# Two stretches of a decoder step written out as lists of steps: from the pool mixer to the second half layer's first Strassen tile, with a third plain tile, and from attention's end to the last half layer's first one

## The chip, the cores and the metric

The kernel runs on one core of one Trainium2 chip. The metric is the device time of one execution in microseconds (us); lower is better. Three runs of the kernel before the change took 1669.02, 1671.43 and 1675.51 us; their median is 1671.43 us.

## The reference, cut to what matters

One inference step of a small decoder: 512 prompt tokens and 8 sample tokens (520 columns), width 1024, hidden width 2816, two layers. Each layer is half a SwiGLU channel mixer, a token mixer, and another half channel mixer, each behind its own root-mean-square norm:

```python
x = x + 0.5 * _swiglu(_rmsnorm(x, norm_g[l, 0]), ffn_w_gate[l, 0], ffn_w_up[l, 0], ffn_w_down[l, 0])
h = _rmsnorm(x, norm_g[l, 1])
# layer 0: out = causal means of h over windows 2, 4, 8, 16, less h, times pool_w, times pool_scale
# layer 1: out = sliding-window attention with sinks on shared keys and values, times w_o
x = x + out
x = x + 0.5 * _swiglu(_rmsnorm(x, norm_g[l, 2]), ffn_w_gate[l, 1], ffn_w_up[l, 1], ffn_w_down[l, 1])
```

So there are four "half layers" (channel mixers), numbered 0 to 3; the pool mixer stands between 0 and 1, the shared keys and values and half layer 2 follow 1, and attention stands between 2 and 3. Outputs are the final norm of x and the new caches. Everything is float32.

## The kernel before, in words

**Layout and precision.** x is kept transposed: eight tiles of 128 channels by 520 tokens. Each float32 operand of a product is split into a high part in TensorE's faster format and the rest as a low part (ScalarE copies the high part, VectorE subtracts: L192 and L193 for weights, L345 and L346, L348 and L349 for activations). Each product is then three matmuls (L519, L545): high by high, high by low, low by high. The norm's factor per token is not applied to x but to the result, as a row R that is multiplied in later, so products can begin before the norm is known.

**A half layer** (`ffn`, L672) makes 22 tiles of 128 hidden channels in three parts of 8, 8 and 6 (`PARTS`), and after each part multiplies with the down weights and adds into x (L711, L712). A hidden tile is gate times up. The first `NPL[fi]` tiles of half layer fi are plain (`plain_tile`, L577): 8 blocks of 128 channels, 3 terms, gate and up, 2 halves of the tokens, which makes 96 matmuls. The others are Strassen tiles (`strassen_tile`, L614): gate and up for both halves of the channels are taken as seven products of 12 matmuls, 84 in all. A Strassen tile needs sums of the weights (two accumulating DMAs from GpSimd's queue, L156 and L157, and two VectorE adds, L162 and L166) and sums of the activations (`sums`, L649: four t12 and four t34 tiles, each split again at L345 and L346). The activations' sums are made once per half layer, while its plain tiles are multiplied; the first Strassen tile waits for them. `NPL` is (3, 2, 2, 2).

**Weights** (`Weights`, L96) come in chunks of 1 MB through three buffers, by DMAs on SyncE's queue (L359). A chunk's buffer is free when all its items are split. `prefetch` (L233) splits five items ahead.

**Start of a half layer.** Half layers 1 and 3 start with `start_hooks` (L732): after each group of four blocks a hook is called, which in turn sums the squares over channels with matmuls against ones (`rstd_tok`, L477), takes the root on VectorE in 12 short instructions (`root`, L486), spreads it over the partitions (`rstd_all`, L500), and makes the activations' sums step by step. `copied` and `known` (L569, L571) copy a plain tile out of PSUM where R is not yet there.

**Pool mixer** (L1008 to L1102). For each of four channel groups, five token blocks are multiplied with pool_w (`zt`, 30 matmuls at L1029), scaled by the norm and split (`zt_evac`, L1033; the scale needs the root), and multiplied with band matrices that hold the means' windows (`band`, L1040, 22 matmuls and 4 short ones). The result goes into x (L1064 for samples, L1067 for the prompt), and x, scaled, is split into the next half layer's operand. The squares for the next norm come after the last group, and eight transposes (L1097) make the pool's state for the output. The sum of squares for the mixer's own norm must hold x of all eight blocks, and the last comes out of half layer 0's last down product.

**Order.** Outside of lists, the framework places instructions by its own timeline estimate, each engine in one in-order queue. Attention, the very beginning and the very end are already written as lists: a `Steps` object (L237) takes steps with an engine, a cost, a due time, what they come after, and which buffer slots they take; it plans them by those numbers, and inside `manual_schedule` the steps go out in exactly that order on TensorE, VectorE, ScalarE and GpSimd. The planner's numbers fix the order and nothing else: on the chip each queue waits for what it needs.

Of the kernel before, what the change touches and what calls it, by code (L numbers as in the profile page):

```python
# [11 lines left out]
F32 = mybir.dt.float32  # L12
# [18 lines left out]
NPL = (3, 2, 2, 2)  # L31
# [64 lines left out]
class Weights:  # L96
# [4 lines left out]
    def __init__(self, nc, rawp, splp, chunks_ahead, ahead):  # L101
        self.nc, self.rawp, self.splp = nc, rawp, splp
        self.ca, self.ahead = chunks_ahead, ahead
        self.chunks, self.items = [], []
        self.nl = self.na = self.ns = self.ng = 0
        self.late = None

# [34 lines left out]
    def sums(self, ch, again):  # L142
# [28 lines left out]
        self.last()  # L171
        self.piece(ch, s2)
        self.piece(ch, lambda raw: blk(raw, 1, 2))
        self.piece(ch, s4)
# [24 lines left out]

    def hi(self, new=None):  # L200
# [3 lines left out]
        src = it[1](self.chunks[it[0]][1])  # L204
# [14 lines left out]
        def ahead(i=self.ns):  # L219
            held = any(c < it[0] for c, _, _ in self.items[i + 1 : i + 3])  # L220
            self.load(it[0] + self.ca - held)
            self.add_up(it[0] + 1)
# [81 lines left out]
def yoco_step(ctx, tc, ins, outs):  # L304
# [148 lines left out]
    N_KV, N_FIN, N_PS = 6, 7, 8  # L453
    r_tok = cp.tile([P, 8], F32, name="r_tok")
# [217 lines left out]
    def ffn(fi, tmp, mov, hooks, tt, tags, after, before_last=None, given=None, end=None):  # L672

        j = 0
        for pi, n in enumerate(PARTS):
            last = pi == len(PARTS) - 1
            hs = Hidden(tags)
            for _ in range(n):
                if given is not None:
                    given(hs)  # L680
                    given = None
                elif j < NPL[fi]:
# [10 lines left out]
            for m0 in range(0, KT, 2):  # L693
# [13 lines left out]
                for m in (m0, m0 + 1):  # L707
# [5 lines left out]
                    if last:  # L713
                        if before_last is not None:
                            next(before_last, None)
                        after(m)

# [3 lines left out]
    def deferred(n, tmp, tag, tags, lst, w=TOK):  # L721


        def f(k):
            z = pair(tags, [P, w])
            split(tuple(a[:, :TOK] for a in z), x[k], gcol(n, k))
            lst.append(z)
            square(k, tmp, tag)
# [22 lines left out]
    with ff_pool() as tmp:  # L751
# [174 lines left out]
        def first_tile(hs):  # L926
# [8 lines left out]
            copied.append(rest)  # L935

# [22 lines left out]
        sel = cp.tile([P, 34], F32, name="sel")  # L959
        sts = cp.tile([P, KT, NS], F32, name="sts")  # L960
# [45 lines left out]
        ffn(0, tmp, mov0, first_hooks(), tt, HH, deferred(1, tmp, "g", XX, mov1, TW), pool_prep(), first_tile)  # L1006

    with tc.tile_pool(name="pm", bufs=2) as pm:  # L1008
        for k in range(KT):
            split(tuple(z[:, TOK:TW] for z in mov1[k]), sts[:, k, :])  # L1010

        tok0 = (0, 128, 256, 384, 400)
        r5 = pm.tile([P, 1], F32, name="r5", bufs=1)

        def zt(gi):

            pd = duo()
            banks = [pd[:, 0, :], pd[:, 1, :], ps()]
            wh, wl = prep["w", gi]
            views = []  # L1020
            for tau in range(5):
                o = banks[tau // 2][:, (tau % 2) * 256 : (tau % 2) * 256 + 256]
                views.append(o)
                n = 0
                for kk in range(2):
                    xh, xl = mov1[2 * gi + kk]
                    s = slice(tok0[tau], tok0[tau] + P)
                    for a, b in ((xh, wh), (xh, wl), (xl, wh)):
                        T.matmul(o, a[:, s], b[:, kk, :], start=(n == 0), stop=(n == 5))  # L1029
                        n += 1  # L1030
            return views

        def zt_evac(views):  # L1033
            zh = pm.tile([P, 5, 256], F32R, tag="zh", name="zh")
            zl = pm.tile([P, 5, 256], F32R, tag="zl", name="zl")
            for tau in range(5):
                split((zh[:, tau, :], zl[:, tau, :]), views[tau], r_tok[:, tau : tau + 1] if tau < 4 else r5)
            return zh, zl

        def band(gi, zz):  # L1040

            zh, zl = zz
            Gt, (th, tl) = prep["G", gi], (prep["T", gi][:, 0, :], prep["T", gi][:, 1, :])
            G = lambda c: Gt[:, B_G + c : B_G + c + 256]
            for mi in range(2):
                m = 2 * gi + mi
                c = slice(mi * P, (mi + 1) * P)
                pd = duo()
                po, pso = pd[:, 0, :], pd[:, 1, :]
                pl = [(0, zh, th), (0, zl, th), (0, zh, tl), (1, zh, G(0)), (1, zl, G(0))]  # L1050
                pr = [(1, zh, G(256)), (1, zl, G(256)), (2, zh, G(128)), (2, zl, G(128)), (3, zh, G(0)), (3, zl, G(0))]
                for half, lst in ((0, pl), (1, pr)):
                    for i, (tau, z, b) in enumerate(lst):
                        T.matmul(  # L1054
                            po[:, half * 256 : half * 256 + 256],
                            z[:, tau, c],
                            b,
                            start=(i == 0),
                            stop=(i == len(lst) - 1),
                        )  # L1060
                bs = Gt[:, B_S : B_S + NS]
                T.matmul(pso[:, :NS], zh[:, 4, c], bs, start=True, stop=False)
                T.matmul(pso[:, :NS], zl[:, 4, c], bs, start=False, stop=True)
                V.scalar_tensor_tensor(  # L1064
                    x[m][:, SP:], pso[:, :NS], gcol(N_PS, m), x[m][:, SP:], op0=ALU.mult, op1=ALU.add
                )
                V.scalar_tensor_tensor(  # L1067
                    x[m][:, :SP], po, gcol(N_PS, m), x[m][:, :SP], op0=ALU.mult, op1=ALU.add
                )
# [889 lines left out]
```

## Time and profile before

| | |
|---|---|
| median of 3 runs | 1671.43 us (1669.02 to 1675.51) |
| the profiled execution's own time | 1674.94 us |
| its span, first to last instruction | 1673.1 us |
| its granted TensorE clock | 0.992 of full |
| DVE, ACT and POOL busy | 1254.4, 884.6 and 175.2 us |
| HBM over the span | 111 GB/s |

In the profile PE is TensorE, PEld its weight loads, DVE VectorE, ACT ScalarE, POOL GpSimd and SP SyncE; a q behind the name is the engine's queue of waits and DMA issues. A row "engine line <- other line: 3.4, 1, 3.4" means 3.4 us of waiting in total, once, 3.4 at the longest. The table of windows gives for each stretch its length, the busy time of each engine with the number of instructions, the granted TensorE clock (PEclk), the busy share of the DMA engines and GB/s. The chain of waits lists pieces as start, length, engine, tile, line and count. "ps" is any pair of PSUM banks; "wh" and "wl" are a weight item's high and low part, "th" and "tl" those of the activations' sums.

### The profile page before, as it was taken

The page shows a single profiled execution, that of the slowest core. Times are in us where ns is not written, and L with a number is a line of the kernel's source. Part 1 is how long each engine was busy: PE and PEld are TensorE (multiplying, and loading weights), DVE is VectorE, ACT ScalarE, POOL GpSimd, SP SyncE. Part 2 cuts the span into 40 slices and gives each one's busy share as a digit, 9 for nine tenths or more (in the row PEclk, how much of TensorE's full clock was granted, in tenths as well). Part 3 has the DMA queues.
Part 4 walks back from the last instruction along what each step waited for, and adds up shares of the span by engine and source line. Part 5 has one row for each costly group of instructions (what it writes and reads, how often), then busy time and mean ns, then how long its engine had stood idle before and what let it go on. Part 6 is the DMA issues. An engine that isn't in the chain of part 4 may idle for free.

```text
span 1673.1 us, 34561 instructions
## 1 busy us (share of the span) xinstructions
PE 1647.5 (98%) x13802; PEld 1629.3 (97%) x13802; DVE 1254.4 (75%) x2400; ACT 884.6 (53%) x1763; POOL 175.2 (10%) x235
## 2 busy tenths in 40 slices
PE   9999999999899999999999999999999999999997
PEld 9999999999899999999999999999989999999997
DVE  7966866887785785878785785778987785785785
ACT  6643643656662562556562562555875663463463
POOL 1101101000101101100201110100220110110100
PEclk9999999999999999999999999999999999999999
DMA  9546846753466665633666666654142565675641
GB/s 241 133 132 135 182 132 136 175 161 97 93 162 152 139 162 145 142 108 114 154 157 156 135 154 162 139 147 113 27 102 71 112 160 143 141 171 137 141 115 52
DMA packets 318240, 227.08 MB, mean 136 GB/s; under 512 B 9568, under 2 KB 293336, under 8 KB 318038
## 3 DMA queue, kind: packets, MB, share of 16 engines
q1 hardware_dynamic: 291360, 178.50, 38.4%
q0 software_dynamic: 23392, 41.83, 15.5%
q10 hardware_dynamic: 3326, 4.53, 0.9%
q8 instruction: 108, 1.77, 0.4%
q14 instruction: 54, 0.44, 0.1%
HBM read 180.89 MB, written 5.04 MB: 111 GB/s over the span
## 4 chain that ended last, share of the span: by engine, by line
PE 93%; DVE 4%; ACT 1%; DMA 1%; issue 1%; DVEq 0%; ACTq 0%
PE ps L545 47%; PE ps L519 32%; PE pa L519 5%; PE ps L1780 2%; PE p L519 1%; PE pb L1385 1%; PE pc L1456 1%; PE ps L1029 1%; PE pc L1441 1%; DMA pr<-in_bands_dram 1%; PE ps L1054 1%; DVE wl L193 1%; PE ps L483 0%; PE t L809 0%; ACT wh L192 0%
## 5 line engine op out<-in xcount | busy, mean ns | idle before, releaser
L192 ACT ACTIVATE wh<-raw 128x512 fp32r<-128x512 f32 (+1 forms) x690 | 418.1, 622 | 511.4 <-PE ps L519 294.2
L193 DVE TENSOR_TENSOR wl<-raw,wh 128x512 fp32r<-128x512 f32 (+1 forms) x690 | 456.6, 677 | 193.1 <-ACT wh L192 189.5
L545 PE MATMUL ps<-th,wh 128*128 128x260 f32 x1264 | 358.5, 284 | 3.6 <-ACT th L345 1.7
L545 PE MATMUL ps<-tl,wh 128*128 128x260 f32 x1264 | 358.1, 284 | 0.6 <-DVE tl L346 0.6
L545 PE MATMUL ps<-th,wl 128*128 128x260 f32 x1264 | 356.4, 284 | 0.8 <-DVE wl L193 0.8
L545 PEld LDWEIGHTS ps<-th,wh 128*128 128x128 f32 x1264 | 238.9, 189 | 5.0 <-ACT th L345 2.1
L545 PEld LDWEIGHTS ps<-tl,wh 128*128 128x128 f32 x1264 | 239.3, 189 | 1.0 <-DVE tl L346 1.0
L545 PEld LDWEIGHTS ps<-th,wl 128*128 128x128 f32 x1264 | 238.4, 189 | 1.2 <-DVE wl L193 1.2
L519 PE MATMUL ps<-hh,wh 128*128 128x260 f32 x1024 | 206.6, 283 | 0.6 <-ACT vtok L1207 0.6
L519 PE MATMUL ps<-hl,wh 128*128 128x260 f32 x1024 | 207.1, 282 | 0.0
L519 PE MATMUL ps<-hh,wl 128*128 128x260 f32 x1024 | 205.1, 282 | 0.0
L545 PE MATMUL ps<-xh,wh 128*128 128x260 f32 x708 | 199.1, 284 | 2.0 <-ACT wh L192 1.5
L545 PE MATMUL ps<-xl,wh 128*128 128x260 f32 x708 | 198.7, 283 | 0.0
L157 POOL DMA_DIRECT2D raw<-raw x79 | 68.4, 866 | 1241.7 <-DVE wl L193 566.5
L545 PE MATMUL ps<-xh,wl 128*128 128x260 f32 x708 | 195.3, 283 | 1.4 <-DVE wl L193 1.4
L519 PEld LDWEIGHTS ps<-hl,wh 128*128 128x128 f32 x1024 | 158.4, 188 | 0.0
L519 PEld LDWEIGHTS ps<-hh,wh 128*128 128x128 f32 x1024 | 157.0, 188 | 1.0 <-ACT vtok L1207 0.9
L519 PEld LDWEIGHTS ps<-hh,wl 128*128 128x128 f32 x1024 | 157.4, 188 | 0.0
L545 PEld LDWEIGHTS ps<-xh,wh 128*128 128x128 f32 x708 | 133.7, 189 | 2.7 <-ACT wh L192 1.9
L711 DVE TENSOR_TENSOR u<-ps,R 128x520 f32<-128x520 f32 x88 | 61.3, 697 | 97.1 <-PE ps L519 97.1
L545 PEld LDWEIGHTS ps<-xl,wh 128*128 128x128 f32 x708 | 133.8, 189 | 0.0
L545 PEld LDWEIGHTS ps<-xh,wl 128*128 128x128 f32 x708 | 131.8, 189 | 1.8 <-DVE wl L193 1.8
(299 smaller groups left out, 3247.1 us busy)
## 6 DMA issues: line engine op xcount, KB each, us to landing
raw<-in_ffn_w_gate_dram SPq DMA_DIRECT2D x87, 512.0 KB
raw<-in_ffn_w_up_dram SPq DMA_DIRECT2D x87, 512.0 KB
raw<-in_ffn_w_down_dram SPq DMA_DIRECT2D x32, 1024.0 KB
S<-in_ffn_w_up_dram SPq DMA_DIRECT2D x79, 256.0 KB
raw<-raw POOLq DMA_DIRECT2D x79, 256.0 KB, 3.3
S<-raw POOLq DMA_DIRECT2D x79, 256.0 KB, 4.6
raw<-in_ffn_w_down_dram SPq DMA_DIRECT2D x16, 768.0 KB
raw<-in_w_q_dram SPq DMA_DIRECT2D x8, 512.0 KB
```

Of the source, the lines that this page charges most:

```text
L157: G.dma_start(blk(raw, 2, 1), blk(raw, 1, 1), accum_op=ALU.add)
L192: nc.scalar.activation(dh, src, AF.Copy)
L193: nc.vector.tensor_tensor(dl, src, dh.bitcast(F32), op=ALU.subtract)
L519: T.matmul(banks[:, hf, :H], a[:, kk, :], hcols(b, hf), start=(first and i == 0), stop=(last and i == 2),)
L545: T.matmul(bank[:, :H], a[:, kk, :], b, start=(not more and kk == 0 and i == 0), stop=(kk == 3 and i == 2), skip_group_check=more,)
L711: V.tensor_tensor(halves(u), banks[m][:, :, :H], halves(R), op=ALU.mult)
L1029: T.matmul(o, a[:, s], b[:, kk, :], start=(n == 0), stop=(n == 5))
L1054: T.matmul(po[:, half * 256 : half * 256 + 256], z[:, tau, c], b, start=(i == 0), stop=(i == len(lst) - 1),)
L1385: T.matmul(o, q_[rows_, qc], k_[rows_, kc_], start=(i == 0), stop=(i == 2))
L1441: T.transpose(pt[:, o : o + P], vals["sm", t, h, bi][:, e, kt * P : (kt + 1) * P], ident)
L1456: T.matmul(po[rows_, bi * P : (bi + 1) * P], vtok[:, max(b - 1, 0) + kt, v0 : v0 + 64], vals["pp", t, h, bi][:, kt * 256 + e * P : kt * 25 ...
L1780: T.matmul(bank, a[:, k % 3, :], b[:, c0:c1], start=(k == 0 and i == 0), stop=(k == 5 and i == 2))
```

## The change

It does six things.

1. `NPL` becomes (3, 3, 2, 2): half layer 1 has a third plain tile in place of its first Strassen tile.
2. Half layer 0 stops two output blocks early (`stop=6`); those two (m = 6 and 7) become the first steps of a new list. `pool_prep` is advanced twice after m = 4 and m = 5, so that its eight steps still fit.
3. The list holds the two output blocks, the whole pool mixer, the norm and sums for half layer 1, its three plain tiles and the first six of seven products of its first Strassen tile. In it, the mixer's sum of squares takes x of block 7 straight from its square (ten sum matmuls in place of five); the four z groups are multiplied with their order and PSUM places fixed; the band product of a block is one run of 520 columns with one addition into x; the first plain tile alternates gate and up for each channel block k, as soon as that block's operand is split.
4. `begin` (shared by both lists) takes the root with one GpSimd instruction (`pow`) in place of the 12 on VectorE, and writes the activations' sums as single steps. `weight_steps` writes the weight items as steps: the accumulating DMAs (`wa`) come behind the norm's root on GpSimd's queue, and the two VectorE adds become steps of their own (`look`).
5. The last half layer starts with a second list: a Silu call that brings in the activation table first, then `begin` with two plain tiles and six products.
6. The DMAs that copy state and caches in DRAM and load the sinks (one of 448 KB, two of 1016 KB, 17 small ones, on SyncE's queue) are issued before the first list in place of after the pool mixer.

The diff's core:

```diff
-NPL = (3, 2, 2, 2)
+NPL = (3, 3, 2, 2)
...
+            done = 0
+            if given is not None:
+                done = given(hs)
+                given = None
+                j += done
+            for _ in range(n - done):
+                if j < NPL[fi]:
...
-            for m0 in range(0, KT, 2):
+            for m0 in range(0, stop if last else KT, 2):
...
                             next(before_last, None)
+                            if stop < KT and m >= stop - 2:
+                                next(before_last, None)
...
+    def weight_steps(st, first, have, count, due, gate=(), width=lambda i: 4):
...
+            add(f"wa{c}", "POOL", 2.2, due(heads[c][0]) - 4.0, lambda c=c: W.add_up(c), after=after + list(gate))
...
+            if first + i in W.made:
+                add(f"ws{i}", "DVE", 0.14 * n + 0.13, due(i) - 0.2, lambda i=i: W.look(first + i), after=after)
+                after = after + [f"ws{i}"]
+            add(f"wh{i}", "ACT", 0.13 * n + 0.13, due(i) - 0.1, lambda i=i: w_hi(i), after=after, takes=takes)
+            add(f"wl{i}", "DVE", 0.14 * n + 0.13, due(i), lambda i=i: w_lo(i), after=[f"wh{i}"] + ([f"wl{i - 1}"] if i else []))
...
+    def begin(st, fi, n, mov, tmp, tt, first, off, base, need, ready, summed, hidden_list, root_):
...
+        def n_root():
+            nc.gpsimd.tensor_tensor(r_tok[:, :5], vals["v"], minus_half, op=ALU.pow)
...
+        for p in range(npl):
+            order = [(k, o) for k in range(KT) for o in range(2)]
+            if p:
+                order = [(k, o) for k0 in (0, 4) for o in range(2) for k in range(k0, k0 + 4)]
...
+        ups, los = [f"L{k}1" for k in range(4)], [f"L{k}0" for k in range(4)]
+        extra = {0: [f"p{npl - 1}.71"], 1: los + ["s0"], 2: ["cs0", "s1"], 3: ["s2"], 4: ["cs1", "s3"], 5: ["cs2", "s4"] + ups}
...
-        ffn(0, tmp, mov0, first_hooks(), tt, HH, deferred(1, tmp, "g", XX, mov1, TW), pool_prep(), first_tile)
+        hs0 = ffn(0, tmp, mov0, first_hooks(), tt, HH, deferred(1, tmp, "g", XX, mov1, TW), pool_prep(), first_tile, stop=6)
...
+        st = Steps(dict(d=4, w=6, sb=4, sa=2, g=2, t=2, sq=2))
...
+        add("x5", "DVE", 3.0, -100.0)
+        add("y5", "ACT", 2.5, -100.0)
...
+                T.matmul(o, acc[:, lo : lo + P], ones[:, 0:1], start=True, stop=False)
+                T.matmul(o, vals["q", 1, 7][:, lo : lo + P], ones[:, 0:1], start=False, stop=True)
...
+        add("ns", "PE", 1.25, 10.5, norm_sums, after=["q7", "a6"], takes=("d",), reads=[("sq", "q7")])
+        add("nm", "DVE", 0.17, 11.0, norm_mean, after=["ns"], reads=[("d", "ns")])
+        add("nr", "POOL", 1.4, 11.0, norm_root, after=["nm"])
...
-        ffn(1, tmp, mov2, start_hooks(tmp, 2, tt, 2), tt, HH, deferred(N_KV, tmp, "g", XX, movk))
+        ffn(1, tmp, mov2, [], tt, HH, deferred(N_KV, tmp, "g", XX, movk), given=mixed)
...
-        ffn(3, tmp, mov6, start_hooks(tmp, 5, tt, 1), tt, HH, None, end=last_part)
+            st.add("tab", "ACT", 1.4, -50.0, table)
...
+        ffn(3, tmp, mov6, [], tt, HH, None, given=first_part, end=last_part)
```

In the lists, x5 and y5 stand for what VectorE and ScalarE still have queued when the first list begins. PSUM is four pairs of banks (d=4). `s0` to `s5` are the Strassen products: s1 waits for the low parts of all four t12 (L00 to L30), s5 for those of all four t34.

More of the change, by code (lines that the diff above doesn't have):

```diff
@@ L727, in f @@
             lst.append(z)
+            if w > TOK:
+                split(tuple(a[:, TOK:] for a in z), sts[:, k, :])
             square(k, tmp, tag)
@@ L935, in first_tile @@
             copied.append(rest)
+            return 1
         def first_hooks():
@@ new lines, in yoco_step, with mixed @@
+        add("ht", "PE", 0.95, 30.0, h_turn, after=[f"hx{k}" for k in range(KT)], takes=("d",))
+        for a in range(2):
+            add(f"ho{a}", "ACT", 0.6, 32.0, lambda a=a: h_out(a), after=["ht", "nr"], reads=[("d", "ht")])
+        begin(
+            st, 1, 2, mov2, tmp, tt, first, 4, B_DUE(7) + 2, lambda k: [f"yl{k}"], lambda k: [f"xp{k}"], ["sa7"],
+            lambda: out_hs[0], 3.0,
+        )
+        def mixed(hs):
+            out_hs.append(hs)
+            with tc.manual_schedule(
+                engines={mybir.EngineType.PE, mybir.EngineType.DVE, mybir.EngineType.Activation, mybir.EngineType.Pool}
+            ):
+                st.emit()
+            begun(1, 4)
+            return NP + 1
```

529 lines of the change are left out of this document (429 added, 100 removed).

## The prediction

> **What bounds the kernel now.** I read the page first: which engine is busy, and what the chain that ended last consists of.
>
> ```profile
> span 1673.1 us, 34561 instructions
> PE 1647.5 (98%) x13802; PEld 1629.3 (97%) x13802; DVE 1254.4 (75%) x2400; ACT 884.6 (53%) x1763; POOL 175.2 (10%) x235
> ...
> PE 93%; DVE 4%; ACT 1%; DMA 1%; issue 1%; DVEq 0%; ACTq 0%
> ```
>
> TensorE is the bound nearly everywhere: only its work, its pauses and its clock matter. Busy time hides a slow clock, so the table of windows over the two stretches came next; there the count of matmuls in brackets says more than the busy time.
>
> ```profile
> 378.20:385.50 7.30, 7.24 (x36) 7.27 (x37) 3.95 (x17) 4.14 (x13) 1.72 (x2) 0.53 0.72 247
> 385.50:408.50 23.00, 21.66 (x179) 20.95 (x179) 16.48 (x37) 13.36 (x26) 1.14 (x3) 1.00 0.14 40
> 408.50:433.70 25.20, 25.20 (x212) 25.20 (x213) 21.75 (x50) 15.96 (x28) 3.63 (x5) 1.00 0.45 97
> 433.70:450.40 16.70, 11.69 (x69) 10.03 (x68) 13.51 (x27) 11.31 (x22) 0.00 (x0) 0.90 0.06 19
> 450.40:496.90 46.50, 46.50 (x390) 46.50 (x389) 40.10 (x70) 28.07 (x54) 5.22 (x6) 1.00 0.66 158
> 1297.00:1322.10 25.10, 25.10 (x213) 25.10 (x213) 18.31 (x42) 15.93 (x26) 5.30 (x6) 1.00 0.70 143
> 1322.10:1334.40 12.30, 10.41 (x58) 9.39 (x57) 10.17 (x21) 8.15 (x17) 0.00 (x0) 0.72 0.00 1
> ```
>
> At full rate a matmul starts every 46.50 / 390 = 0.119 us. The stretch before the first Strassen product sums (433.7 to 450.4) starts 69, worth 8.2 us: 8.5 of its 16.7 us are lost. The one after attention (1322.1 to 1334.4) starts 58, worth 6.9: 5.4 lost. Last, the chain of waits over the mixer, which gives its work, and who TensorE waited for.
>
> ```profile
> 371.57 1.20 DVE wl L193 x2
> ...
> 374.74 0.60 DVE wl L193
> 375.34 0.62 DVE x L712
> ...
> 378.26 1.86 PE ps L483 x10
> 380.12 9.68 PE ps L1029 x60
> 389.80 1.29 PE ps L1054 x11
> 391.09 0.11 PE ps L1063
> ...
> 392.71 3.67 PE ps L1029 x30
> ...
> 405.55 0.45 PE ps L1097 x4
> ...
> 408.49 11.64 PE ps L519 x96
> 420.13 1.01 PE ps L483 x10
> ```
>
> ```profile
> PE ps L483 <- DVE acc L472: 3.4, 1, 3.4
> ...
> PE ps L545 <- ACT wh L192: 1.1, 1, 1.1
> ...
> PE ps L1054 <- DVE x L1067: 1.1, 1, 1.1
> ```
>
> The mixer at full rate: four z groups of 30 at 3.67 = 14.7, eight bands at 1.29 + 0.11 = 11.2, two transposes' halves 0.9, sums 1.0 (as at 420.13), together 27.8 us. It takes from 371.1 to 408.5, 37.4: 9.6 lost. Of these, 3.4 are the wait for the sum of squares; 3.2 are half clock after it (sums 1.86 for 1.01, sixty z matmuls 9.68 for 7.34); 3.0 are waits between evacuations and bands.
>
> Lost in all: 9.6 + 8.5 + 5.4 = 23.5 us. That is what the change can win.
>
> **The change part by part.**
>
> *Third plain tile.* 96 matmuls for 84: 12 x 0.119 = 1.4 us on the path. Off it, four splits of weights for seven, two VectorE adds and two accumulating DMAs fewer.
>
> *Ten sum matmuls for five in the mixer's norm.* Another row like 420.13: +1.0 us on the path. In return the last addition into acc goes.
>
> *Two output blocks into the list, and the wait for x7.* VectorE is behind here: TensorE was through with block 7 at 371.1, but its x is written at 375.34 + 0.62 = 376.0. Three weight splits for later tiles (1.20 + 0.60) stood ahead of it; by their due times (33 and more after the list's start) the list puts them behind, so x7 comes at 374.2. Its square goes straight into the sums, so they can start at about 375.1. TensorE has by then done four of z's parts of group 0 (about 2.9 us, from 371.1 to 374.0): it waits 1.1 us. If the splits stay ahead, 2.9; if the backlog is gone, 0. I take 1.1, since it is the splits' due times that say where they go. Behind the sums on TensorE's queue stand the other z parts and the bands; ScalarE and VectorE wait for the root anyway.
>
> Does the clock fall after this wait? After 3.4 us it did (0.53 in the row from 378.2); after the 1.1 us wait of L1054 it did not (1.00 in the row from 385.5). 1.1 us lies at the second: nothing, with 3.2 us as the upper end. [...] The row from 433.7 does not wholly agree: its longest wait is 1.1 us, but the clock is 0.90, so many short waits do it as well.
>
> *Root on GpSimd.*
>
> ```profile
> 380.36 0.17 DVE L492 TENSOR_SCALAR ny<-nv 128x5 int32<-128x5 int32 x1
> ...
> 382.37 0.17 DVE L498 SCALAR_TENSOR_TENSOR r_tok<-nt,ny 128x5 f32<-128x5 f32 x1
> ```
>
> ```profile
> L1853 POOL TENSOR_TENSOR r_tok<-nv,minus_half x3: 544/694/1093, 1646.5 to 1666.1; 128x2 f32<-128x2 f32 x2, 8x1 f32<-8x1 f32 x1
> ...
> 421.75 0.90 POOL L157 DMA_DIRECT2D raw<-raw  x1 [12.29 <-DVE ny L493]
> ```
>
> 2.2 us of VectorE become 0.5 to 1.1 us of GpSimd. On the path it counts nothing: sixteen z parts (16 x 0.73 = 11.7 us) lie between the sums and the first band. Without that cover it would be up to 1.1. Its queue also issues the weights' accumulating DMAs; the list puts them behind the root, and their data are needed only at the second Strassen product, three plain tiles later.
>
> *Mixer as a list.* Twenty parts of z are split, x added in one instruction for two, bands run in order. TensorE now has the first plain tile's parts to fill with, one pair as each block is split. Of the 3.0 us between evacuations and bands I take half, 1.5; ends 0 (the cover is complete) and 3.0 (as before).
>
> *Moved copies.*
>
> ```profile
> 374.26 0.85 SPq L1107 DMA_DIRECT2D out_dram<-in_state_pool_dram  x1
> ...
> 377.09 19.71 SPq L1116 DMA_DIRECT2D sink_s<-in_attn_sinks_dram  x16
> ...
> 415.53 0.39 SPq L359 DMA_DIRECT2D raw<-in_ffn_w_gate_dram  x1
> ```
>
> All twenty are issued by 377.09 + 19.71 = 396.8 and the next weight load starts at 415.5. Started some ten us earlier, they pass no weight load that anyone waits for. Nothing; if a load did land behind them, TensorE has five split items in hand.
>
> *Up to the first Strassen tile.* The lost 8.5 us are VectorE's:
>
> ```profile
> L193 DVE TENSOR_TENSOR wl<-raw,wh 128x512 fp32r<-128x512 f32 x11 | 7.6, 689 | 1.7 <-ACT wh L192 1.6
> L346 DVE TENSOR_TENSOR tl<-t,th 128x520 fp32r<-128x520 f32 x8 | 5.6, 696 | 1.8 <-ACT th L345 1.8
> L472 DVE TENSOR_TENSOR acc<-acc,sq 128x520 f32<-128x520 f32 x7 | 4.9, 697 | 0.4
> ```
>
> From 408.5 to 450.4 it is busy 21.75 + 13.51 = 35.3 of 41.9 us, under TensorE work of 25.2 us and one Strassen product. The third tile adds 11.6 us of cover (row 408.49) and about four splits (2.8 us) with two 0.7 us instructions of its gate; the root takes 2.2 away. So 37 us of VectorE stand under some 38 us of TensorE, and the t34 half of the sums (about 6 us) may come 5.8 us later, at product s5. I take 0.8 us left; ends 0 and 4.2 (half of the loss).
>
> *After attention.* The same without a third tile.
>
> ```profile
> 1313.20 1.28 ACT L603
> ...
> 1328.65 0.64 ACT wh L192
> ```
>
> The table load (1.28) and a weight split stood in the chain; the list loads the table first, while TensorE has its first blocks, and takes t12's splits before t34's. VectorE has 18.3 us busy in the 25.1 us before, so there is room. I take 1.0 of 5.4 left; ends 0 and 2.7.
>
> *Sum.* Lost before 23.5; left 1.1 + 1.5 + 0.8 + 1.0 = 4.4; added 1.4 + 1.0 = 2.4. The gain is 16.7 us. The profiled execution took 1674.94 us (its span and 1.8 around it), so it would take 1658.2. It lies 3.5 us above the median of 1671.43, from which the forecast is 1671.4 - 16.7 = 1654.7.
>
> **The rivals.**
>
> *The wait moves along.* VectorE's backlog at the list's start is larger than the list allows for (3.0 us at x5), and fixed order hands it on. TensorE waits 2.9 at the sums, the clock falls (3.2), and the bands keep their 3.0: the mixer keeps 9.1 of 9.6. Gain 23.5 - 9.1 - 1.8 - 2.4 = 10.2: 1661.2. For it: block 7's x came 4.9 us after its product. Against: three splits leave the way.
>
> *VectorE stays the bound.* 37 us under 38 leaves no room for an order that is a little off. Then 6 of the 8.5 us stay, and 4 of the 5.4, since fixed order cannot fill a hole: 23.5 - 2.6 - 6 - 4 - 2.4 = 8.5: 1662.9. Against: t34 can wait.
>
> *The lists say what the framework did.* If order was not the cause, the pauses stay and the extra work is added: 1671.4 + 2.4 = 1673.8. Against: the table load and the three splits are matters of order.
>
> *Slower: the clock stays at half.* The first plain tile now alternates by block, each pair waiting for its own split, so pauses are many and short, as in the row from 433.7. At 0.53 the row from 378.2 starts a matmul every 7.24 / 36 = 0.201 us, 0.082 more than at full rate. If half clock lasts from the sums through two plain tiles (120 + 88 + 192 = 400 matmuls), that is 32.8 us: 1654.7 + 32.8 = 1687.5. It decides from (1679.8 - 1654.7) / 0.082 = 306 matmuls on. Against: such spells were 3.4 to 7 us long so far. [...]
>
> **How the numbers follow.** The forecast has 0.60; the wait that moves 0.17; VectorE as bound 0.12; no effect 0.05; slower 0.06. A measurement of this kernel tells 0.5%, 8.4 us, from no change, so faster means under 1663.1. All of the forecast, two thirds of the second case and half of the third lie there: 0.60 + 0.12 + 0.06 = 0.78. Same is the rest of those and the fourth: 0.16. Slower 0.06. With no residue the gain is 21.1 (1650.3), a little under that with the runs' scatter; on the other side the range takes in the second and third case: 1649.5 to 1664.5.
>
> **What would show it right or wrong.** Right: in the mixer one wait of about 1 us ahead of the sums and no clock under 1 from the sums on; from the mixer's first z to s1 a count of matmuls over time near 0.12 us each; ahead of s1 no wait over 0.5 us on t12's splits; GpSimd's root under 1.1 us; after attention no clock under 1, and the table load gone from the chain. Wrong: a wait of 3 us or more ahead of the sums; half clock in the first plain tile; a wait for R or for PSUM in the second plain tile, because the root stands behind an accumulating DMA; new waits at the border to the tiles that the framework orders.

## The result, and the profile after

The changed kernel takes 1657.32 us (median, 1656.62 to 1657.60); the kernel before, run beside it on the same chip, takes 1670.22 (1667.08 to 1675.51). The ratio is 0.9921, 95% interval 0.9901 to 0.9941: faster by 12.9 us, 0.8%. The forecast was 1654.7.

The page of the changed kernel, its span, its first row of engines and the chain that ended last. The profiled execution took 1656.62 us.

```profile
span 1654.8 us, 34551 instructions
...
PE 1637.9 (99%) x13824; PEld 1623.0 (98%) x13824; DVE 1241.1 (75%) x2350; ACT 878.9 (53%) x1756; POOL 178.0 (11%) x237
...
PE 94%; DVE 3%; DMA 1%; ACT 1%; issue 0%; SPq 0%; DVEq 0%; ACTq 0%
```

TensorE has 22 matmuls more than before (13824 for 13802), which are the 12 of the third tile and the 10 of the sums, and is 9.6 us less busy all the same, at least in part because less of its time is at half clock: the granted clock is 0.996 of full for 0.992, some 6 us over the span.

To see where the 18.3 us between the two spans (1673.1 and 1654.8) went, I counted the matmuls of both traces from their ends and compared when the same matmul starts. (The 22 extra ones lie ahead of the stretch that is aligned this way; ahead of them I counted from the front.)

| stretch | before less after, at its end | gained in the stretch |
|---|---|---|
| start of the program, to 342 us | 0.9 | 0.9 |
| first list: two output blocks, mixer, plain tiles, to the first Strassen tile | 13.6 | 12.7 |
| from there to the end of attention | 11.9 | -1.7 |
| second list: from attention to the first Strassen tile | 17.6 | 5.7 |
| the rest | 18.1 | 0.5 |

So the two lists gained 18.4 us in this pair of executions. The table of windows of the changed kernel over the same stretches (columns as before: TensorE's busy time and matmuls in brackets first, the granted clock third from the right):

```profile
374.08:377.49 3.41, 2.82 (x24) 2.82 (x25) 1.31 (x3) 2.58 (x6) 0.00 (x0) 1.00 0.35 135
377.49:380.90 3.41, 3.41 (x19) 3.41 (x17) 1.78 (x6) 0.29 (x1) 1.57 (x1) 0.50 0.03 3
380.90:402.00 21.10, 21.05 (x182) 20.99 (x181) 17.84 (x37) 16.47 (x35) 2.16 (x4) 1.00 0.22 56
...
415.00:439.00 24.00, 24.00 (x202) 24.00 (x201) 18.46 (x33) 13.87 (x26) 5.32 (x6) 1.00 0.73 152
439.00:455.00 16.00, 16.00 (x136) 16.00 (x135) 11.61 (x20) 9.91 (x20) 1.75 (x2) 1.00 0.35 85
1284.00:1310.00 26.00, 26.00 (x221) 26.00 (x220) 21.23 (x41) 18.90 (x32) 6.87 (x7) 1.00 0.60 136
1310.00:1330.00 20.00, 20.00 (x170) 20.00 (x169) 16.40 (x28) 12.01 (x24) 1.77 (x3) 1.00 0.52 106
```

From 380.9 on, as far as the two stretches go, TensorE is hardly ever idle (21.05 of 21.10, 24.00 of 24.00, 16.00 of 16.00), at clock 1.00, where before it lost 8.5 us ahead of the first Strassen sums and 5.4 after attention. One disturbed place is left, from 374 to 381: a pause, and 3.41 us at clock 0.50. The chain of waits shows what stood ahead of the sums:

```profile
369.30 0.53 ACT wh L221
369.86 0.69 DVE wl L225
370.55 0.69 DVE xl L1319
371.24 0.61 DVE acc L1337
371.92 0.68 DVE wl L225
372.60 0.62 DVE u L1308
373.25 0.71 DVE x L1311
373.98 0.65 ACT sq L1330
374.67 0.38 PE ps L1347 x2
```

Block 7's x (L1311) still has two weight splits (L225, 0.69 and 0.68) ahead of it. The list's own numbers put them there: x5 stands for 3.0 us that VectorE has queued when the list begins, it has more, and the planner used time that did not exist. Later the chain is TensorE alone, here up to the first Strassen tile and after attention:

```profile
415.85 23.20 PE ps L530 x192
439.06 31.01 PE ps L556 x259
```

```profile
1293.84 16.66 PE ps L530 x138
1310.49 21.53 PE ps L556 x180
```

The plain tiles (L530) run straight into the Strassen sums (L556), the second and third plain tile at 23.20 / 192 = 0.121 us a matmul, with no split, table load or gate step between. Two of the waits that TensorE still has:

```profile
PE ps L1649 <- DVE u L724: 1.1, 1, 1.1
...
PE ps L1347 <- ACT sq L1330: 0.7, 1, 0.7
```

The second is the pause at the sums. The first, at 1120 us where attention begins and so between the two stretches, explains most of the -1.7 in the table; in a second profile of the same kernel (1656.23 us) it is not there.

### The profile page after: what moved, and what is told of

Read it like the earlier page. It is cut to its first block, busy times and chain, and to the rows that moved or that the text cites. A ratio compares the mean times of both kernels' runs of the same rounds, so it can differ in the third digit from the quotient of the medians.

```text
span 1654.8 us, 34551 instructions
## 1 busy us (share of the span) xinstructions
PE 1637.9 (99%) x13824; PEld 1623.0 (98%) x13824; DVE 1241.1 (75%) x2350; ACT 878.9 (53%) x1756; POOL 178.0 (11%) x237
## 4 chain that ended last, share of the span: by engine, by line
PE 94%; DVE 3%; DMA 1%; ACT 1%; issue 0%; SPq 0%; DVEq 0%; ACTq 0%
PE ps L556 47%; PE ps L530 34%; PE pa L530 5%; PE ps L2196 2%; PE pb L1801 1%; PE pc L1872 1%; PE pc L1857 1%; PE p L530 1%; PE ps L1375 1%; PE ps L1412 1%; DMA pr<-in_bands_dram 1%; DVE wl L225 0%; DMA raw<-in_ffn_w_gate_dram 0%; DVE xl L358 0%; DMA pr<-in_pool_w_dram 0%
## 5 line engine op out<-in xcount | busy, mean ns | idle before, releaser
L195 ACT ACTIVATE wh<-raw 128x512 fp32r<-128x512 f32 (+1 forms) x658 | 398.1, 622 | 486.9 <-PE ps L530 287.2
L196 DVE TENSOR_TENSOR wl<-raw,wh 128x512 fp32r<-128x512 f32 (+1 forms) x658 | 434.8, 677 | 180.3 <-ACT wh L195 177.1
L556 PE MATMUL ps<-th,wh 128*128 128x260 f32 x1248 | 352.0, 282 | 1.0 <-DVE sb L649 0.8
L556 PE MATMUL ps<-tl,wh 128*128 128x260 f32 x1248 | 352.2, 282 | 0.0
L556 PE MATMUL ps<-th,wl 128*128 128x260 f32 x1248 | 350.7, 282 | 0.0
L556 PEld LDWEIGHTS ps<-th,wh 128*128 128x128 f32 x1248 | 234.6, 188 | 1.4 <-DVE sb L649 1.0
L556 PEld LDWEIGHTS ps<-tl,wh 128*128 128x128 f32 x1248 | 234.7, 188 | 0.0
L556 PEld LDWEIGHTS ps<-th,wl 128*128 128x128 f32 x1248 | 234.2, 188 | 0.0
L530 PE MATMUL ps<-hh,wh 128*128 128x260 f32 x1024 | 206.5, 283 | 0.6 <-ACT vtok L1623 0.6
L530 PE MATMUL ps<-hl,wh 128*128 128x260 f32 x1024 | 207.1, 282 | 0.0
L530 PE MATMUL ps<-hh,wl 128*128 128x260 f32 x1024 | 205.0, 282 | 0.0
L556 PE MATMUL ps<-xh,wh 128*128 128x260 f32 x696 | 195.0, 282 | 0.6 <-ACT sb L639 0.6
L556 PE MATMUL ps<-xl,wh 128*128 128x260 f32 x696 | 195.0, 282 | 0.0
L556 PE MATMUL ps<-xh,wl 128*128 128x260 f32 x696 | 191.5, 282 | 0.0
L530 PEld LDWEIGHTS ps<-hl,wh 128*128 128x128 f32 x1024 | 158.4, 188 | 0.0
L530 PEld LDWEIGHTS ps<-hh,wh 128*128 128x128 f32 x1024 | 157.0, 188 | 0.9 <-ACT vtok L1623 0.9
L530 PEld LDWEIGHTS ps<-hh,wl 128*128 128x128 f32 x1024 | 157.3, 188 | 0.0
L556 PEld LDWEIGHTS ps<-xh,wh 128*128 128x128 f32 x696 | 130.8, 188 | 0.8 <-ACT sb L639 0.8
L556 PEld LDWEIGHTS ps<-xl,wh 128*128 128x128 f32 x696 | 131.0, 188 | 0.0
L530 PE MATMUL ps<-xl,wh 128*128 128x260 f32 x640 | 130.2, 283 | 0.0
```

The costliest lines, as they stand in the source:

```text
L195: nc.scalar.activation(dh, src, AF.Copy)
L196: nc.vector.tensor_tensor(dl, src, dh.bitcast(F32), op=ALU.subtract)
L530: T.matmul(banks[:, hf, :H], a[:, kk, :], hcols(b, hf), start=(first and i == 0), stop=(last and i == 2),)
L556: T.matmul(bank[:, :H], a[:, kk, :], b, start=(not more and kk == 0 and i == 0), stop=(kk == 3 and i == 2), skip_group_check=more,)
```

## The experiments

The theory: order did it. VectorE's work was done in an order that kept TensorE waiting at three places, and these pauses halved the clock; the two lists put it in the right order, and the third plain tile, the root on GpSimd and the copies' place matter little. The main rival: the third tile is the cover without which VectorE stays the bound, as the prediction had it. Times are medians; each ratio is against the kernel before on the same chip (its medians there: 1669.63, 1670.31, 1670.44 and 1671.01 us).

**How far one execution may be trusted.** before_again is the kernel before, profiled once more.

> The kernel before, profiled a second time. Theory (the first profiled execution was an unlucky one): it took 1674.94 us where the median is 1670.2, and its half-clock spells (6.8 us in the mixer, 3.4 us before the first Strassen tile, 6.8 us after attention) are longer than usual. Then this execution takes 1667 to 1671 us, and the lost matmul time in the two stretches is 3 to 5 us under the 23.5 of the first profile. Rival (the change loses something that its profile doesn't show): the same 23.5 us lost in the two stretches.

It took 1672.49 us. TensorE's wait at the mixer's sums:

```profile
PE ps L483 <- DVE acc L472: 2.1, 1, 2.1
```

2.1 us for the 3.4 of the first profile, with one window of half clock (3.41 us) behind it for two. So this loss varies from one execution to the next, and the prediction's table took a large one. Matched matmul by matmul with the first profile, this one saves 3.1 us in the mixer and next to nothing in the rest of the two stretches, so some 20.4 of the 23.5 us were lost again. The execution as a whole still lay above the median (1669.63), so it does not show how much a usual one loses. changed_again is the changed kernel once more.

> The changed kernel once more, as the measure for the three others on the same chip: 1657 to 1658 us. Its wait ahead of the mixer's sums (1.0 us in the first profile) is expected to differ from one execution to the next, 0.5 to 2.5 us, as the backlog of VectorE at the list's start does.

1656.94 us, ratio 0.9923 (0.9908 to 0.9938): the gain repeats. The wait at the sums is 1.1 us here, and two windows of half clock follow it (377.00 to 383.83 us) where the first profile has one.

**Each list alone.** list_a_only gives the last half layer back to the framework:

```diff
-        ffn(3, tmp, mov6, [], tt, HH, None, given=first_part, end=last_part)
+        ffn(3, tmp, mov6, start_hooks(tmp, 5, tt, 1), tt, HH, None, end=last_part)
```

> Only the first list with the third plain tile; the last half layer starts as before. Theory (two stretches, each with its own pauses): the mixer and first tiles as in the changed kernel, the stretch after attention as before with about 5 us lost, so 4 to 6 us slower than the changed kernel, 1661.5 to 1663 us. Rival (gains overlap, since an execution's clock depends on what went before): the second list adds nothing, 1657 to 1658 us.

1663.42 us, ratio 0.9963 (0.9950 to 0.9977). TensorE's waits after attention are back:

```profile
PE ps L556 <- DVE wl L196: 1.1, 1, 1.1
PE ps L556 <- ACT wh L195: 1.0, 2, 0.6
```

list_b_only is the kernel before with the second list alone; its main lines against the changed kernel:

```diff
-NPL = (3, 3, 2, 2)
+NPL = (3, 2, 2, 2)
...
-        ffn(1, tmp, mov2, [], tt, HH, deferred(N_KV, tmp, "g", XX, movk), given=mixed)
+        ffn(1, tmp, mov2, start_hooks(tmp, 2, tt, 2), tt, HH, deferred(N_KV, tmp, "g", XX, movk))
```

> Only the second list (last half layer); mixer, NPL and half layer 1 as before. Theory: 4 to 6 us under the kernel before, 1664 to 1666 us. Rival (the framework's order had the same waits in its power): no change, 1669 to 1671 us.

1665.28 us, ratio 0.9978 (0.9965 to 0.9991). So the first list is worth 6.2 us in medians, the second 4.4, both together 12.9 to 13.4. They add up to a little less than both, which the intervals allow.

**Is the third plain tile cover, or cost?** two_plain is the changed kernel with one line back:

```diff
-NPL = (3, 3, 2, 2)
+NPL = (3, 2, 2, 2)
```

> Both lists, but two plain tiles in half layer 1 (NPL 3, 2, 2, 2). Theory (the third tile is cover for VectorE): the 1.4 us of twelve matmuls are saved, but TensorE waits for t12's splits before the second Strassen product, 3 to 8 us: 1659 to 1664 us. Rival (order alone did it): the tile is a pure cost, and without it the kernel takes 1655.5 to 1656.5 us.

1656.52 us, ratio 0.9916 (0.9903 to 0.9930): not slower, though in its profile the pause at the mixer's sums (2.1 us) and the half clock behind it (6.83 us) are longer than in the changed kernel's. Its windows from the mixer on:

```profile
376.00:402.00 26.00, 24.88 (x185) 24.82 (x186) 17.41 (x41) 15.87 (x35) 3.58 (x4) 0.87 0.37 92
...
415.00:439.00 24.00, 24.00 (x204) 24.00 (x203) 18.75 (x37) 15.02 (x29) 4.90 (x5) 1.00 0.57 122
439.00:455.00 16.00, 16.00 (x136) 16.00 (x135) 14.45 (x26) 9.28 (x19) 1.75 (x2) 1.00 0.64 139
```

Its Strassen products begin at 431.59 us and TensorE does not wait: 24.00 of 24.00 with VectorE busy 18.75, 16.00 of 16.00 with 14.45. With the list's order two tiles are enough. The reverse, third_only, is the kernel before with the third tile and nothing else (NPL = (3, 3, 2, 2)).

> The kernel before with NPL 3, 3, 2, 2 and nothing else, so the framework orders three plain tiles. Forecast's step (VectorE is short of cover ahead of the first Strassen tile): the 8.5 us lost there go, 1.4 us are added, so 1663 to 1666 us. Rival (the order of the sums is what costs, whatever the cover): the loss stays and 1.4 us are added, 1670.5 to 1672 us.

1669.80 us, ratio 1.0000 (0.9989 to 1.0012): nothing gained. Its waits from the mixer to the Strassen products:

```profile
PE ps L483 <- DVE acc L472: 3.8, 1, 3.8
PE ps L545 <- ACT th L345: 2.1, 1, 2.1
PE ps L545 <- DVE tl L346: 1.2, 1, 1.2
```

The pauses moved behind the third tile (to 450 us) and stayed. Cover without the list bought at most its own 1.4 us; the lists without cover bought all of the gain.

**What halves the clock at the sums?** late_sums tells the list's planner of VectorE's real backlog, so that the sums come behind more z work:

```diff
-        add("x5", "DVE", 3.0, -100.0)
-        add("y5", "ACT", 2.5, -100.0)
+        add("x5", "DVE", 6.5, -100.0)
+        add("y5", "ACT", 5.0, -100.0)
```

> The changed kernel with the planner told of VectorE's and ScalarE's true backlog at the first list's start (x5 6.5 for 3.0, y5 5.0 for 2.5), so that the sums come after more of z on TensorE's queue and one weight split less stands ahead of block 7's x. Theory (fixed order hands the backlog on as a wait and as half clock): no wait ahead of the sums, no clock under 1 in the mixer, 1.5 to 3 us less than the changed kernel. Rival (the wait is only moved to the root's readers, the z evacuations): same time within 0.7 us, a wait of 1 to 2 us ahead of the first band.

1658.52 us, ratio 0.9926 (0.9909 to 0.9943): no gain. The theory that the short wait halves the clock fell here, and the trace says why. First its windows, then the groups of matmuls in the first of the two:

```profile
375.22:378.64 3.42, 3.42 (x33) 3.42 (x32) 0.83 (x2) 1.42 (x4) 0.00 (x0) 1.00 0.13 39
378.64:382.05 3.41, 3.39 (x16) 3.10 (x16) 1.78 (x6) 1.22 (x4) 1.57 (x1) 0.50 0.03 3
```

```profile
L1347 PE MATMUL ps<-ones,sq 128*128 128x1 f32 x10 | 1.8, 250 | 0.0
L1346 PE MATMUL ps<-ones,acc 128*128 128x1 f32 x10 | 1.7, 242 | 0.0
```

The wait is gone, TensorE is busy 3.42 of 3.42 us, and the clock is halved in the next window all the same. But 20 of its matmuls are one column wide (128x1): they fill 2.1 us of TensorE's time and take the place of full-width ones, of which 11 start in this window. The busy share misleads elsewhere too: of the rows shown, 374.08 of the changed kernel is busy 2.82 of 3.41 us, with 6 full-width matmuls started, and half clock follows; 381.19 of five_sums_two (below) is busy only 2.19 of 3.42, all of it full-width, and the clock stays. late_sums_two is the same with two plain tiles (NPL = (3, 2, 2, 2)).

> The same with two plain tiles in half layer 1 (NPL 3, 2, 2, 2). Theory now (the list alone covers the sums, the third tile is twelve matmuls too many): 1.0 to 1.8 us less than late_sums. Rival (the third tile is cover that the earlier run without it did not need by chance): same or slower than late_sums.

1655.39 us, ratio 0.9909 (0.9892 to 0.9925): 3.1 us under late_sums by the medians, with overlapping intervals. In its profile there is a wait of 1.2 us at the sums and one window of half clock behind them. five_sums_two takes half of these one-column matmuls away from it (as in the kernel before, VectorE adds block 7's square into acc):

```diff
-                T.matmul(o, acc[:, lo : lo + P], ones[:, 0:1], start=True, stop=False)
-                T.matmul(o, vals["q", 1, 7][:, lo : lo + P], ones[:, 0:1], start=False, stop=True)
+                T.matmul(o, acc[:, lo : lo + P], ones[:, 0:1], start=True, stop=True)
...
-        add("ns", "PE", 1.25, 10.5, norm_sums, after=["q7", "a6"], takes=("d",), reads=[("sq", "q7")])
+        add("a7", "DVE", 0.7, 9.6, lambda: sum_of(1, 7), after=["q7", "a6"], reads=[("sq", "q7")])
+        add("ns", "PE", 0.62, 10.5, norm_sums, after=["a7"], takes=("d",))
```

> Block 7's square is added to the running sum on VectorE, as in the kernel before, and the sums are five one-column matmuls, not ten; the due times and the two plain tiles are those of late_sums_two. Theory, the clock is halved because the matmuls of one column, with the short wait among them, leave the array nearly empty for long enough: the sum comes 0.7 us later, but TensorE has parts of z to do meanwhile, and the 3.4 us of half clock behind the sums are gone, so the time falls by 1.0 to 2.5 us to some 1653 to 1654.5. Rival, the clock is halved by something else (the switch to transposes or to short matmuls of 120 columns behind): half clock stays near 378 us, and the time lies within 1 us of 1655.4.

1653.42 us, ratio 0.9897 (0.9882 to 0.9912). The time agrees with the theory, though the intervals of this and of late_sums_two overlap; the clock is plain. Its windows, and TensorE's waits in the mixer:

```profile
374.37:377.78 3.41, 3.38 (x30) 3.20 (x29) 2.55 (x5) 3.04 (x7) 0.00 (x0) 1.00 0.37 153
377.78:381.19 3.41, 2.54 (x22) 2.34 (x21) 1.11 (x5) 0.20 (x1) 1.57 (x1) 1.00 0.04 1
381.19:384.61 3.42, 2.19 (x19) 2.01 (x18) 2.77 (x9) 3.42 (x11) 0.00 (x0) 1.00 0.23 60
```

```profile
PE ps L1372 <- ACT hh L1385: 1.2, 1, 1.2
PE ps L1372 <- DVE nv L1347: 0.9, 1, 0.9
```

It waits more than the changed kernel does (1.2 and 0.9 us), yet the clock stays at 1.00: each of these windows starts 17 full-width matmuls or more.

**Root on GpSimd.** dve_root puts it back on VectorE in both lists:

```diff
-            nc.gpsimd.tensor_tensor(r_tok[:, :5], v, minus_half, op=ALU.pow)
+            root(vals["f", 0][:, 1, :5])
...
-        add("nm", "DVE", 0.17, 11.0, norm_mean, after=["ns"], reads=[("d", "ns")])
-        add("nr", "POOL", 1.4, 11.0, norm_root, after=["nm"])
+        add("nr", "DVE", 2.4, 11.0, norm_root, after=["ns"], reads=[("d", "ns")])
```

> The changed kernel with the root of both lists back on VectorE, where it is several instructions of some 2.4 us in all, in place of one power on GpSimd. Theory (the place of the root costs or brings nothing, for TensorE has other matmuls meanwhile): within 1.5 us of 1657. Rival (GpSimd's power is a part of the gain, for VectorE has no room in the stretch where it is the busiest after TensorE): 2 to 4 us slower than the changed kernel, 1659 to 1661, with waits on VectorE behind the sums.

1659.79 us, ratio 0.9938 (0.9923 to 0.9952): some 2.5 us slower than the changed kernel, with overlapping intervals. The waits that the rival wanted are not behind the sums but at the second list's far end, 1349 us:

```profile
PE ps L556 <- ACT sa L642: 1.3, 1, 1.3
PE ps L556 <- DVE sb L649: 0.3, 1, 0.3
```

Matched matmul by matmul, the profile falls 2.5 us behind the changed kernel's between 1327 and 1355 us, and by no more than 0.5 us at a time in the rest of the lists. That VectorE's root there is the cause is likely, not shown. The run also answers a rival to order, that the lists gain because they give VectorE less to do (1241.1 us busy for 1254.4): the roots put 5.0 of these 13.3 us back (1246.1), and 10.6 us of gain are left by the medians (1659.79 for 1670.44). The merged additions into x, 1.7 us of VectorE by their durations, were not tried alone.

**The moved copies.** copies_after meant to issue the twenty transfers behind the first list, by moving their lines behind the place where it is written out.

```diff
-    later(nc.sync.dma_start(pool_sample[0, :, 0:14, :], state_pool[0, :, 1:15, :]))
...
             begun(1, 4)
+            later(nc.sync.dma_start(pool_sample[0, :, 0:14, :], state_pool[0, :, 1:15, :]))
...
```

> The changed kernel with the twenty moved transfers issued behind the first list, as the kernel before has them behind the mixer, and not ahead of it. Theory, as forecast (they cost nothing at either place): within 1 us of 1657. Rival (ahead of the list they hold SP's queue while weight pieces and x wait for it, which is where the wait ahead of the sums comes from): 1 to 2 us faster, with no gap ahead of the sums. The other rival (behind the list they come late for the attention): 1 to 3 us slower, with a wait where the attention takes the window.

1668.28 us, ratio 0.9986 (0.9976 to 0.9995), outside of all three expectations. The chain near the program's start, then TensorE's longest wait:

```profile
15.69 1.75 SPq L1522
...
18.24 16.28 DMA out_dram<-in_cache_v_win_dram
34.53 4.84 DMA S<-in_ffn_w_up_dram
```

```profile
PE ps L494 <- DVE acc L1084: 5.9, 1, 5.9
```

The framework, which orders SP's queue, put them not behind the list but at 15.7 us, ahead of the first layer's weights: a weight piece waited for a 1 MB copy of 16.28 us, and TensorE 5.9 us for VectorE, with 10.2 us of half clock around it. So this run does not test the place that it was meant to test; it shows what a bad place costs, 11 us. copies_late is five_sums_two with the lines after the whole half layer, where SP's queue holds them behind its weights.

```diff
-    later(nc.sync.dma_start(pool_sample[0, :, 0:14, :], state_pool[0, :, 1:15, :]))
...
         ffn(1, tmp, mov2, [], tt, HH, deferred(N_KV, tmp, "g", XX, movk), given=mixed)
+    later(nc.sync.dma_start(pool_sample[0, :, 0:14, :], state_pool[0, :, 1:15, :]))
...
```

> five_sums_two with the twenty moved transfers behind the whole second half layer in SP's order (after its last weight pieces, where the attention's first pieces follow), no longer ahead of the first list's. Theory, as forecast (where the changed kernel issues them, from 361 us, no weight and no x waits for them, so their place costs nothing): within 1.5 us of five_sums_two's 1653.4, the gaps from 340 to 460 us the same within 0.5 us in all; and, as the sums are five here too, no half clock right behind them. Rival (at 361 to 381 us they delay pieces that the first list waits for): 1.5 to 3 us faster, with the gaps near 379 and 384 us gone.

1652.53 us, ratio 0.9895 (0.9878 to 0.9912), as five_sums_two (0.9897): in the time, the place ahead of the list costs nothing that these runs can tell. The traces show more. The chain in five_sums_two, behind its sums:

```profile
364.78 14.19 DMA sraw<-in_attn_sinks_dram
...
379.07 0.16 DVE nsinks L1561
379.23 0.08 DVE nv L1347
...
379.39 1.58 POOL r_tok L1350
```

The sinks (sraw) are issued behind the two 1 MB copies and land 14.19 us later; VectorE's two instructions that use them (nsinks, L1561) stand ahead of the norm's mean (nv) in its queue, so the mean, the root and what hangs on them wait. In copies_late they no longer stand there: TensorE's wait for nv is 0.3 us for 0.9, and its gaps near 379 and 384 us, from start to start of matmuls, are 0.5 and 1.5 us for 1.1 and 1.5. That is half a microsecond, under what the times resolve. The clock is full behind five sums here too:

```profile
376.17:379.58 3.41, 3.16 (x27) 2.91 (x25) 1.92 (x6) 2.09 (x6) 0.00 (x0) 1.00 0.03 9
```

These last two are the fastest versions, by medians some 4 to 5 us below the changed kernel: two plain tiles, five sums, and a planner that knows VectorE's backlog.

## Why the prediction was right, and where it was not

**The three losses: right.** It found 23.5 us lost in two stretches and called them matters of order. The same stretches gained 12.7 and 5.7 us in the profiles, 18.4 after the added work of 2.4; in the medians each list alone gained 6.2 and 4.4.

**What stays in the mixer: right in size by luck, wrong in kind.** Forecast were 1.1 us of wait at the sums, no half clock, and 1.5 us at the bands. The wait at the sums is 0.7 us; the bands keep nothing (21.05 of 21.10 us busy); in place of that there is one window of half clock. In it 17 full-width matmuls start for 29, so it costs 12 x 0.119 = 1.4 us. 2.1 us are left for 2.6. In changed_again the wait is 1.1 us and the half clock lasts twice as long, so there the mixer keeps more than was forecast.

**"It is the splits' due times that say where they go": half wrong.** Two weight splits still stand ahead of block 7's x, because a due time moves a step back only as far as the planner believes VectorE to be busy. It cost little that the times can tell: late_sums, without the wait, is no faster.

**"The third tile adds 11.6 us of cover": the step that failed.** It set 37 us of VectorE against 38 of TensorE and concluded that the tile was needed; two_plain has no wait with a tile less, and third_only gains nothing with a tile more. The sum put all of VectorE's work from 408.5 us on under the plain tiles, as the framework had it. The list starts part of it earlier, under the mixer. VectorE's queue in the kernel before, then in two_plain:

```profile
412.54 2.30 DVE L472 TENSOR_TENSOR acc<-acc,sq 128x520 f32<-128x520 f32 x3
...
426.99 0.70 DVE L346 TENSOR_TENSOR tl<-t,th 128x520 fp32r<-128x520 f32 x1 [0.58 <-ACT th L345]
```

```profile
401.43 0.70 DVE L1337 TENSOR_TENSOR acc<-acc,sq 128x520 f32<-128x520 f32 x1
...
414.03 0.69 DVE L848 TENSOR_TENSOR tl<-t,th 128x520 fp32r<-128x520 f32 x1
```

The additions of squares begin 11.1 us earlier and the low parts of the activations' sums 13.0 us, while the first Strassen product begins at nearly the same time (433.7 and 431.6 us). By then seven of the eight low parts have begun, where three had before. So the mixer was the cover that the sum left out. The tile gains nothing; by the medians of the two pairs of kernels that differ in it alone it costs 0.4 us (changed_again and two_plain, on two chips) and 3.1 us (late_sums and late_sums_two), within overlapping intervals, where its 12 matmuls alone would be 1.4.

**"Does the clock fall after this wait? ... nothing": wrong.** Half clock follows the ten sums in these profiles: 3.41 us at 0.50 in the changed kernel and in late_sums, 6.83 us in changed_again and two_plain, and a granted clock of 0.83 from 380 to 400 us in copies_after. The prediction compared lengths of waits; in the traces the half clock goes with how few full-width matmuls start in the 3.41 us ahead of it: 0, 9 and 12 in the kernel before, 6 in the changed kernel (the last section has the rows). It lasts 3.41 or 6.83 us at a time in the two stretches of these two profiles, and 10.2 us once in copies_after. In late_sums it came without a wait: a window without a gap, 3.42 of 3.42 us busy, has 0.50 behind it.

**Root on GpSimd: right for the path, wrong for the duration.**

```profile
L1353 POOL TENSOR_TENSOR r_tok<-nv,minus_half x1: 1572/1572/1572, 379.0 to 379.0; 128x5 f32<-128x5 f32 x1
```

1.57 us, where 0.5 to 1.1 was forecast from narrower operands. The z parts hide it in the changed kernel. In five_sums_two, with fewer z parts left at that time, TensorE does wait for what hangs on it (hh, 1.2 us).

**"Moved copies ... Nothing": right for the time, by luck of a cover that it didn't name.** It looked for a weight load behind them and found none; it did not look for who uses their data. VectorE's nsinks came along, from 428.6 us before to 378.0 in the changed kernel, and wait there:

```profile
DVE nsinks L1563 <- DMA sraw<-in_attn_sinks_dram: 1.9, 1, 1.9
```

Behind them in VectorE's queue stands the norm's mean. In the changed kernel ninety z matmuls (376.84 to 389.08) lie over it and TensorE doesn't wait; in five_sums_two, with fewer left, it waits 0.9 us.

**Table load, borders: right.** The table load is gone from the chain after attention; no wait for R or PSUM came in the later plain tiles. The 1.1 us at 1120 us was one execution's.

**The sum.** 23.5 - 2.1 - 2.4 = 19.0 us, against 18.4 in the profiles, and yet 12.9 in the medians: the profiled execution of before lay 4.7 us above its median (1674.94 and 1670.22), that of after 0.7 below its own (1656.62 and 1657.32). So the forecast of 16.7 was too low for the pair of executions that it was worked out from and too high for the medians. Taking a sum found in an execution above the median off the median was its main error in size: some of the losses found in it, 3.1 us of the mixer by before_again, are not in every execution.

## What to carry to other kernels

Where TensorE pauses while another engine has room on average, look at the order of that engine's queue before adding cover: order gained here what a tile of cover didn't, and an order written out by hand is only as good as the backlog that it assumes at its start. Size a forecast from more than one execution of the kernel before, or check its largest terms for how much they vary. And of a moved DMA, look up where it ends up in its queue and who uses its data, not where its line stands.

## What the runs showed of the hardware

The first profiles of the two kernels show, window by window, what went ahead of the half clock. In both stretches (340 to 470 and 1270 to 1380 us) its spells are 3.41 or 6.83 us long there, so the windows are 3.41 us, laid to begin and end with these spells. Counted are the matmuls that start in each: those 256 or 260 columns wide (full-width) and those of one column. Where TensorE works without a pause at full clock, 28 or 29 full-width ones start in a window (before, 450.39 to 467.46 us). The windows in which the clock was halved, those ahead of them, and some with few starts:

| kernel, window from (us) | TensorE busy, us | full-width started | one-column started | clock | clock of the next window |
|---|---|---|---|---|---|
| before, 371.88 | 2.97 | 23 | 0 | 1.00 | 1.00 |
| before, 375.29 | 0.45 | 0 | 5 | 1.00 | 0.50 |
| before, 378.71 | 3.41 | 10 | 5 | 0.50 | 0.50 |
| before, 382.12 | 3.41 | 16 | 0 | 0.50 | 1.00 |
| before, 436.73 | 2.02 | 13 | 0 | 1.00 | 1.00 |
| before, 440.15 | 2.18 | 11 | 0 | 1.00 | 1.00 |
| before, 443.56 | 1.69 | 9 | 0 | 1.00 | 0.50 |
| before, 446.97 | 3.42 | 16 | 0 | 0.50 | 1.00 |
| before, 1324.20 | 2.02 | 12 | 0 | 1.00 | 0.50 |
| before, 1327.61 | 2.92 | 10 | 0 | 0.50 | 0.50 |
| before, 1331.03 | 3.41 | 16 | 0 | 0.50 | 1.00 |
| changed, 370.66 | 3.26 | 25 | 2 | 1.00 | 1.00 |
| changed, 374.08 | 2.82 | 6 | 18 | 1.00 | 0.50 |
| changed, 377.49 | 3.41 | 17 | 0 | 0.50 | 1.00 |

In these rows half clock comes behind 0 to 10 full-width starts and once behind 12, full clock behind 11 and behind 13 or more. They are fourteen windows of two executions and give no limit: 11 and 12 fell on opposite sides. What fills the rest differs, waiting in the kernel before at 443.56 us, one-column sums in the changed kernel at 374.08 and in late_sums at 375.22 (11 full-width started, 20 of one column, 0.50 behind it). A window at half clock costs about 1.5 us, an estimate from the rows: 16 or 17 starts for 28 or 29 are 12 or 13 fewer, at 0.119 us each.

The 2.1 us of one-column sums fell into these windows differently from one execution to the next, which is likely one reason why executions differ: in the changed kernel 18 of them start in one window in the first profile, with one window of half clock behind, and 17 and 3 in two windows in changed_again, with two. That it is the width, and not something else about those sums, rests on the full window of late_sums and on late_sums_two against five_sums_two; the widths between were not tried.
